# A reserve of filler work, and a later start of the filler, in the attention of a two-layer decoder

## The chip, the cores and the metric

The program runs on one core of one Trainium2 chip. The metric is the device time of one execution in microseconds (us). A core has five engines that work beside each other: TensorE (PE in the profile, with PEld for its weight loads) for matrix products and transposes into PSUM, VectorE (DVE), ScalarE (ACT), GpSimd (POOL) and SyncE (SP), which here only issues DMAs. Each engine takes its instructions strictly in the order in which the built program lists them; a waiting instruction holds up all that stands behind it on its engine.

## The reference

Two decoder layers over 1024 tokens of width 1024, in float32. Layer 0 mixes with retention and mLSTM heads, layer 1 with sparse attention (16 heads in 4 groups) and an S5 state-space branch. Around them:

```
for i in range(DEPTH):
    u = rmsnorm(h, norm_pre[i])
    y = ab_mixer(u, ...) if i % 2 == 0 else cd_mixer(u, ...)
    h = h + rmsnorm(y, norm_post[i])
    h = h + jax.nn.sigmoid(h @ pe_gate[i]) * (p[i] @ pe_proj[i])

def cd_mixer(...):
    y_nsa = nsa(...) * silu(nz)             # compressed, selected and sliding-window attention
    y_s5 = s5(...) * silu(sz)               # s5 ends in z1 * sigmoid(z2), (z1, z2) = y @ w_glu
    mix = concat([y_nsa, y_s5])
    return mix @ w_out                      # cd_w_out, 1536 x 1024
```

The change is about `p[1] @ pe_proj[1]` (below: p Wp), which depends on inputs alone, and about when it and the other products around the attention are computed.

## The kernel before

Every float32 product is made of three: an operand is split into a high and a low part, and TensorE multiplies high by high, high by low and low by high (`mm`, L139, is the line of nearly all matmuls, so tiles tell them apart).

**The attention of layer 1** is a loop over 32 units, a unit being a group of four heads and one tile of 128 tokens: group 0 from tile 7 down to 0, groups 1 and 2 from 0 to 7, group 3 in the order `LAST` = 7, 6, 5, 0, 1, 2, 3, 4. A unit makes scores (`sc`, L1425 takes mask and maximum on VectorE, L1428 the exponential on ScalarE, L1440 and L1442 scale on ScalarE, VectorE or GpSimd), then values: for each 128 keys four transposes (`pt`, L1485), a high part (`pthh`, ScalarE L1476), a low part (`pthl`, VectorE L1477) and two products into `av`. The unit's end takes `av` out through ScalarE and VectorE (L1654, L1655) and multiplies it with the gate `zn`.

**The filler** is a Python generator, `filler`, whose steps are put between the attention's instructions, behind the matmul named by `pace` and at a lower priority; a scheduler then fixes each engine's order. `step(gg, n)` adds `share[gg] * n / 66` to a credit and takes a step of the filler for each whole credit; a group's shares are thus its number of steps. In order, the steps are:

- the S5 branch's GLU: 16 steps of 24 matmuls 256 wide (`gl`);
- the S5 half of the output product (`W2` rows from 1024): 16 steps of 12 matmuls 512 wide (`fp`), stored to `yD`;
- p Wp: per token tile a step that loads 128 rows of p and transposes them (`ft`, two transposes, split by ScalarE L1497 and VectorE L1498), and two steps of 6 `fp` matmuls, copied by ScalarE (L1571) and stored to `ppD`, which only the gate stage reads;
- the output product of groups 0 and 1 (16 steps of 12 `fp`), then of group 2 (16 steps of 6 `fp`), added to `yD`; a step whose attention output isn't there yet is a bare `yield`, which costs a credit and does nothing;
- the **last chain**, for tiles 7, 6, 5, 0, 1, 2, 3: load the two halves of `yD` (L1587), two products of 6 `fp` with group 3's output, VectorE adds each (L1592), ScalarE squares it (L1593), VectorE and GpSimd (L226) make the norm's factor, ScalarE scales (L1601), GpSimd multiplies by the norm's gain (L1602) and adds the residual (L1603) for each half, and SyncE stores to `hD` (L1604).

All filler products go through one PSUM buffer (`pF`), so a product waits until the one before has been read. Results go through a ring of four half tiles (tag `fo`), other inputs through another ring of four (`fin`).

**The gate stage** follows: its weights, its tile loads `h<-hD` (L934; the first two are issued from ScalarE's queue), transposes `trp`, products `gp`, and p Wp read back from `ppD`.

Of the kernel before, what the change touches and what calls it, by code (L numbers as in the profile page):

```python
# [97 lines left out]
def body(tc, A, out, dbg=None):  # L98
# [1058 lines left out]
    with ExitStack() as e:  # L1157
# [252 lines left out]
        pace = [None]  # L1410
# [55 lines left out]
    with ExitStack() as e:  # L1466
# [23 lines left out]

        def filler():

# [26 lines left out]

            wg = weights(A["s5_w_glu"][0], 0, 4)  # L1520
            for l0 in range(0, 8, 2):
                hi = pf.tile([128, 4, 256], FR, name="fhi", tag="fhi")
# [5 lines left out]
                for m in range(4):  # L1528
# [16 lines left out]
                    yield  # L1545
            for src, w, kt0, nk, dst, add in ((None, W2, 8, 4, yD, False),
                                              (A["p"][1, 0], A["pe_proj"][1], 0, 2, ppD, False),
                                              (mixN, W2, 0, 4, yD, True),
                                              (mixN, W2, 4, 2, yD, True)):
                wq = weights(w, kt0, nk)  # L1550
                for i in range(NT):
                    while src is mixN and not all((q, i) in ready for q in ((0, 1) if kt0 == 0 else (2,))):
                        yield
                    x = ftile()
                    to = dst[i * 128:(i + 1) * 128, :]
                    if src is None or src is mixN:
                        x = x.rearrange("p (a k) -> p a k", a=4)[:, :nk]
                        if src is None:
                            to = dst.rearrange("(k l) c -> l k c", l=8)[i]
                            nc.sync.dma_start(x, mixS[:, i, :].rearrange("(a p) k -> p a k", p=128))  # L1560
                        else:
                            nc.sync.dma_start(x, mixN[kt0:kt0 + nk, :, i * 128:(i + 1) * 128].rearrange("a p k -> p a k"))
                        T = local_parts(x, nk, g)
                    else:
                        nc.sync.dma_start(x[:, :nk * 128], src[i * 128:(i + 1) * 128, :])
                        T = turn(x, nk)
                        yield
                    for hf in range(2):
                        hs = slice(hf * 512, (hf + 1) * 512)
                        y = ftile("fy", "fo")  # L1570
                        s.activation(y, product(T, wq[hf], nk), AF.Copy, scale=0.25 if src is None else 1.0)  # L1571
                        if add:
                            y0 = ftile()
                            nc.sync.dma_start(y0, to[:, hs])
                            g.tensor_tensor(y, y, y0, op=OP.add)
                        nc.sync.dma_start(to[:, hs], y)
                        yield
            wq = wlast[0] = [[load_w(W2, [(hf * 512, 512)], 6, 2)] for hf in range(2)]
            for i in LAST[:-NL]:
                while (3, i) not in ready:  # L1580
                    yield
                rows = slice(i * 128, (i + 1) * 128)
# [23 lines left out]

        wlast = [None]
        fill = filler()

        credit = [0.0]  # L1610
        share = {0: 30, 1: 26, 2: 20, 3: 64}
        ready = {}

        def step(gg, n):
            credit[0] += share[gg] * n / 66
            while credit[0] > 0.99:
                credit[0] -= 1
                with tc.issue_after(pace[0].ins), tc.high_priority(offset=FOFF):
                    next(fill, None)

        FOFF = -1000
        for n, (gg, i) in enumerate(units):
# [36 lines left out]
            ready[gg, i] = zt  # L1659
        for _ in fill:  # L1660
            pass
    ep.close()
# [66 lines left out]
```

## Time and profile before

| | us |
|---|---|
| runs, undisturbed | 2359.98, 2362.42, 2365.99 (median 2362.42) |
| the profiled execution | 2361.37 |
| its span in the profile | 2359.5 |
| TensorE busy | 2272.2 (96%) |
| VectorE busy | 1468.9 (62%) |
| ScalarE busy | 1073.5 (45%) |
| GpSimd busy | 488.4 (21%) |

The attention's units run from 1512 to 2241 us of the span, the gate stage from 2250 to the end. The granted clock of TensorE has two levels in the profile, 1.00 (2.4 GHz) and 0.50 (1.2 GHz). A matmul's listed duration includes its way through the array, so a row of matmuls is read by the distance of their starts.

### The profile page before, as it was taken

The page shows a single profiled execution, that of the slowest core. Times are in us where ns is not written, and L with a number is a line of the kernel's source. Part 1 is how long each engine was busy: PE and PEld are TensorE (multiplying, and loading weights), DVE is VectorE, ACT ScalarE, POOL GpSimd, SP SyncE. Part 2 cuts the span into 40 slices and gives each one's busy share as a digit, 9 for nine tenths or more (in the row PEclk, how much of TensorE's full clock was granted, in tenths as well). Part 3 has the DMA queues.
Part 4 walks back from the last instruction along what each step waited for, and adds up shares of the span by engine and source line. Part 5 has one row for each costly group of instructions (what it writes and reads, how often), then busy time and mean ns, then how long its engine had stood idle before and what let it go on. Part 6 is the DMA issues. An engine that isn't in the chain of part 4 may idle for free.

```text
span 2359.5 us, 34480 instructions
## 1 busy us (share of the span) xinstructions
PE 2272.2 (96%) x11974; PEld 1903.7 (81%) x11974; DVE 1468.9 (62%) x3893; ACT 1073.5 (45%) x2345; POOL 488.4 (21%) x585
## 2 busy tenths in 40 slices
PE   7999999999999999999999999989999989999888
PEld 6888889788888788888888899778888778787667
DVE  6777646755554434443287344278787898888833
ACT  6223323433332432233332233267787777787821
POOL 0222200000000000200000000044444245565700
PEclk9999999999999999999999999999999999999999
DMA  6423312021221645424377424342453433355543
GB/s 160 91 78 107 97 50 72 19 72 29 79 72 37 213 156 198 146 77 138 108 221 239 121 80 141 102 135 71 117 164 116 125 110 105 115 171 156 174 160 111
DMA packets 266695, 279.26 MB, mean 118 GB/s; under 512 B 54384, under 2 KB 200408, under 8 KB 266490
## 3 DMA queue, kind: packets, MB, share of 16 engines
q1 hardware_dynamic: 254666, 243.95, 34.1%
q10 hardware_dynamic: 8240, 24.20, 3.1%
q0 software_dynamic: 3616, 8.92, 1.4%
q8 instruction: 95, 1.56, 0.3%
q14 instruction: 78, 0.64, 0.1%
HBM read 189.84 MB, written 88.42 MB: 118 GB/s over the span
## 4 chain that ended last, share of the span: by engine, by line
PE 83%; DVE 7%; DMA 4%; ACT 2%; issue 2%; SPq 1%; POOL 1%; ACTq 0%; DVEq 0%; POOLq 0%
PE pj L139 42%; PE gp L139 7%; PE op L139 6%; PE fp L139 5%; PE av L139 4%; PE sc L139 4%; PE pt L1485 3%; PE yp L139 2%; PE gl L139 2%; DVE pr L1425 1%; PE trp L214 1%; PE pp L139 1%; DVE pthl L1477 1%; PE cs L139 1%; PE hp L139 1%
## 5 line engine op out<-in xcount | busy, mean ns | idle before, releaser
L139 PE MATMUL pj<-whi,uh 128*128 128x512 f32 (+2 forms) x768 | 278.7, 364 | 2.4 <-DVE z L484 0.9
L139 PE MATMUL pj<-wlo,uh 128*128 128x512 f32 (+2 forms) x768 | 277.9, 362 | 0.0
L139 PE MATMUL pj<-whi,ul 128*128 128x512 f32 (+2 forms) x768 | 277.7, 362 | 0.0
L1428 ACT ACTIVATE pr<-pr,nm 128x640 f32<-128x640 f32 (+7 forms) x256 | 187.3, 732 | 66.4 <-DVE nm L1425 63.6
L139 PE MATMUL pj<-vh,whi 128*128 128x512 f32 x512 | 203.9, 399 | 0.2 <-ACT vh L218 0.2
L139 PE MATMUL pj<-vl,whi 128*128 128x512 f32 x512 | 201.3, 393 | 0.0
L139 PE MATMUL pj<-vh,wlo 128*128 128x512 f32 x512 | 201.1, 393 | 0.0
L164 DVE SCALAR_TENSOR_TENSOR wlo<-raw,gnp,whi 128x256 fp32r<-128x256 f32 (+3 forms) x264 | 144.8, 586 | 75.3 <-ACT whi L163 74.5
L1477 DVE TENSOR_TENSOR pthl<-pt,pthh 128x512 fp32r<-128x512 f32 x264 | 177.4, 683 | 16.3 <-ACT pthh L1476 14.1
L163 ACT ACTIVATE whi<-raw,gnp 128x256 fp32r<-128x256 f32 (+3 forms) x264 | 138.0, 585 | 79.6 <-PE pj L139 38.3
L139 PE MATMUL op<-whi,mhl 128*128 128x512 f32 x520 | 165.4, 395 | 2.7 <-ACT mhl L218 1.9
L1476 ACT ACTIVATE pthh<-pt 128x512 fp32r<-128x512 f32 x264 | 149.8, 592 | 37.4 <-PE pt L1485 34.5
L139 PEld LDWEIGHTS pj<-whi,uh 128*128 128x128 f32 x768 | 145.6, 190 | 25.7 <-PE trp L214 1.1
L1485 PE MATMUL pt<-consts,pr 128*128 128x128 f32 x1056 | 161.8, 277 | 4.3 <-ACT pr L1440 2.1
L139 PEld LDWEIGHTS pj<-wlo,uh 128*128 128x128 f32 x768 | 145.7, 190 | 22.7 <-issue 0.7
L139 PEld LDWEIGHTS pj<-whi,ul 128*128 128x128 f32 x768 | 145.4, 189 | 22.4 <-issue 0.2
L139 PE MATMUL gp<-whi,mhl 128*128 128x512 f32 x480 | 155.3, 399 | 0.0
L1485 PEld LDWEIGHTS pt<-consts,pr 128*128 128x128 f32 x1056 | 130.8, 142 | 28.5 <-ACT pr L1440 3.1
L139 PE MATMUL sc<-kh,q 128*128 128x320 f32 (+5 forms) x384 | 141.4, 371 | 9.2 <-DVE nm L1425 7.7
L1442 POOL TENSOR_SCALAR pr<-pr,cf 128x640 f32<-128x640 f32 (+4 forms) x64 | 114.8, 1793 | 154.9 <-DVE cf L1437 65.3
L139 PE MATMUL sc<-kl,q 82*128 82x320 f32 (+5 forms) x384 | 126.9, 333 | 0.0
L139 PE MATMUL av<-pthl,vt 128*128 128x512 f32 x264 | 115.0, 436 | 9.8 <-DVE pthl L1477 9.4
(444 smaller groups left out, 5546.5 us busy)
## 6 DMA issues: line engine op xcount, KB each, us to landing
raw<-in_ab_w_in_dram SPq DMA_DIRECT2D x100, 256.0 KB
raw<-in_cd_w_in_dram SPq DMA_DIRECT2D x30, 512.0 KB
yD<-fy SPq DMA_DIRECT2D x48, 256.0 KB
raw<-in_ab_w_out_dram SPq DMA_DIRECT2D x16, 512.0 KB
raw<-in_pe_gate_dram SPq DMA_DIRECT2D x16, 512.0 KB
qD<-qst SPq DMA_DIRECT2D x16, 512.0 KB
q<-qD SPq DMA_DIRECT2D x32, 256.0 KB
fin<-yD SPq DMA_DIRECT2D x32, 256.0 KB
```

The costliest lines, as they stand in the source:

```text
L139: return t.matmul(o, l, r, start=start, stop=stop, **k)
L163: s.activation(hi[:, k], raw[:, k], AF.Copy, scale=gain(kt0 + k))
L164: v.scalar_tensor_tensor(lo[:, k], raw[:, k], gain(kt0 + k), hi[:, k].bitcast(FT), op0=OP.mult, op1=OP.subtract)
L214: t.transpose(ps[:, k * 128:(k + 1) * 128], x[:, (k4 + k) * 128:(k4 + k + 1) * 128], ident)
L1425: v.tensor_tensor_reduce(pr[:, x:y], ps[:, :y - x], mask[:, x:y], op0=OP.add, op1=OP.min, scale=-1.0, scalar=nm[:, 0:1] if c else 3e38, ac ...
L1428: s.activation(pr[:, :nk], pr[:, :nk], AF.Exp, scale=-1.0, bias=nm[:, c:c + 1], accum_out=sums[:, b, h:h + 1])
L1442: (v if eng == "v" else g).tensor_scalar(P[h][:, :nk], P[h][:, :nk], cf[:, h:h + 1], None, op0=OP.mult)
L1476: s.activation(hi[:dst_shape], ps[:dst_shape], AF.Copy)
L1477: v.tensor_tensor(lo[:dst_shape], ps[:dst_shape], hi[:dst_shape].bitcast(FT), op=OP.subtract)
L1485: t.transpose(ps[:, h * 128:(h + 1) * 128], P[h][:, k * 128:(k + 1) * 128], ident)
```

## The change

The filler becomes two generators. `filler(True)`, the reserve (`extra`), has p Wp alone; `filler()` has the rest. The transposing step of p Wp loses its own `yield`, so a tile of p Wp is two steps. Where the main filler's inputs are missing it now yields `False`: no credit is spent on that, and `step` instead takes two steps of the reserve for two credits, if the main filler has come to its narrow weights (those of group 2's product, `nk == 2`) or the reserve has begun; if the reserve can't be drawn on, the loop stops and the credit is kept. The credit starts at -2.5, and the shares of the four groups go from 30, 26, 20, 64 to 20, 16, 18, 53. What is left of both generators runs after the loop.

```
-        def filler():
+        def filler(spare=False):
...
-            wg = weights(A["s5_w_glu"][0], 0, 4)
-            for l0 in range(0, 8, 2):
+            wg = None if spare else weights(A["s5_w_glu"][0], 0, 4)
+            for l0 in range(0, 0 if spare else 8, 2):
...
-            for src, w, kt0, nk, dst, add in ((None, W2, 8, 4, yD, False),
-                                              (A["p"][1, 0], A["pe_proj"][1], 0, 2, ppD, False),
-                                              (mixN, W2, 0, 4, yD, True),
-                                              (mixN, W2, 4, 2, yD, True)):
+            for src, w, kt0, nk, dst, add in (((A["p"][1, 0], A["pe_proj"][1], 0, 2, ppD, False),) if spare else
+                                              ((None, W2, 8, 4, yD, False), (mixN, W2, 0, 4, yD, True),
+                                               (mixN, W2, 4, 2, yD, True))):
                 wq = weights(w, kt0, nk)
+                narrow.append(nk == 2)
                 for i in range(NT):
                     while src is mixN and not all((q, i) in ready for q in ((0, 1) if kt0 == 0 else (2,))):
-                        yield
+                        yield False
...
                         T = turn(x, nk)
-                        yield
...
+            if spare:
+                return
             wq = wlast[0] = [[load_w(W2, [(hf * 512, 512)], 6, 2)] for hf in range(2)]
             for i in LAST[:-NL]:
                 while (3, i) not in ready:
-                    yield
+                    yield False
...
-        wlast = [None]
-        fill = filler()
-
-        credit = [0.0]
-        share = {0: 30, 1: 26, 2: 20, 3: 64}
+        wlast, narrow = [None], []
+        fill, extra = filler(), filler(True)
+
+        credit = [-2.5]
+        share = {0: 20, 1: 16, 2: 18, 3: 53}
...
         def step(gg, n):
+
             credit[0] += share[gg] * n / 66
             while credit[0] > 0.99:
+                with tc.issue_after(pace[0].ins), tc.high_priority(offset=FOFF):
+                    if next(fill, False) is False:
+
+                        if not any(narrow) or next(extra, False) is False or next(extra, False) is False:
+                            break
+                        credit[0] -= 1
                 credit[0] -= 1
-                with tc.issue_after(pace[0].ins), tc.high_priority(offset=FOFF):
-                    next(fill, None)
...
-        for _ in fill:
-            pass
+        for x in (fill, extra):
+            for _ in x:
+                pass
```

In the changed kernel's listing the lines of the filler move down by one or two: L1497 and L1498 become L1498 and L1499, L1509 becomes L1510, L1587 to L1604 become L1589 to L1606, L1654 becomes L1661.

**The start of the filler, ScalarE.** The values of the first unit (`pthh`), with the first inputs of the GLU (`fin`) ahead of them. Before:

```order
L1440 ACTIVATE pr<-pr,cf 128x1024
L1134 ACTIVATE zt<-pj 128x512
L159 ACTIVATE whi<-raw 128x1024 x2
L1370 ACTIVATE scc<-scc 128x4x48
L1497 ACTIVATE fhi<-fin 128x4x128 x2
L1476 ACTIVATE pthh<-pt 128x512 x3
```

And now:

```order
L1440 ACTIVATE pr<-pr,cf 128x1024
L1134 ACTIVATE zt<-pj 128x512
L159 ACTIVATE whi<-raw 128x1024 x2
L1370 ACTIVATE scc<-scc 128x4x48
L1498 ACTIVATE fhi<-fin 128x4x128 x2
L1476 ACTIVATE pthh<-pt 128x512 x3
```

Nothing has moved here but a line number. On TensorE at this place the first `gl` matmuls go from the first unit's values to behind them.

**The end of the attention, TensorE.** The last product of the last unit and what follows it (`trp` and `gp` are the gate stage's). Before:

```order
L139 MATMUL av_23343<-pthl_23450,vt_19023 128x512
L214 MATMUL trp_23531<-consts_75,h1_23528 128x128 x4
L214 MATMUL trp_23538<-consts_75,h1_23528 128x128 x4
L139 MATMUL gp_23579<-whi_23481,mhl_23530 128x512
L139 MATMUL gp_23579<-wlo_23482,mhl_23530 128x512
```

And now, where `fp_22830` is the first of five products of the last chain:

```order
L139 MATMUL av_23198<-pthl_23334,vt_18848 128x512
L139 MATMUL fp_22830<-whi_21553,fhi_22720 128x512
L139 MATMUL fp_22830<-wlo_21554,fhi_22720 128x512
L139 MATMUL fp_22830<-whi_21553,flo_22721 128x512
L139 MATMUL fp_22830<-whi_21553,fhi_22720 128x512
```

All 30 matmuls of those five products follow the last `av`, then five times two `ft` and 12 `fp`, and only then `trp`.

**The same place, ScalarE.** Before, from the last `av` being taken out (`oc`) to the first loads of the gate stage:

```order
L1654 ACTIVATE oc_23455<-av_23343 64x256
L1601 ACTIVATE fy_23242<-fy_23242,rsb_23325 128x512
L1601 ACTIVATE fy_23243<-fy_23243,rsb_23325 128x512
L934 DMA h1_23528<-hD2_98 128x1024
L934 DMA h1_23545<-hD2_98 128x1024
```

And now the end of the last chain (tile 3) and the first of the five reserve tiles:

```order
L1595 ACTIVATE fin_23175,ms2_23105<-fy_23098 128x512
L1603 ACTIVATE fy_23097<-fy_23097,rsb_23180 128x512
L1603 ACTIVATE fy_23098<-fy_23098,rsb_23180 128x512
L1498 ACTIVATE fhi_23260<-ft_23257 128x2x128
L1571 ACTIVATE fy_23264<-fp_23265 128x512
L1571 ACTIVATE fy_23274<-fp_23275 128x512
```

Four more reserve tiles (L1498 and two of L1571 each) and two weight splits (L159) follow before the two loads of L934.

## Rows read from the trace of the kernel before

**Rows 1.** Busy time by stretch: attention by groups, group 3 in two parts.

```profile
core 0: us, PE busy (x) PEld busy (x) DVE busy (x) ACT busy (x) POOL busy (x), PEclk, DMA share, GB/s
1512.00:1721.00 209.00, 193.88 (x1241) 170.83 (x1239) 159.33 (x485) 141.73 (x322) 87.96 (x87) 0.96 0.42 118
1721.00:1898.00 177.00, 170.61 (x957) 143.50 (x957) 144.36 (x451) 135.91 (x294) 65.94 (x70) 0.99 0.40 124
1898.00:2074.00 176.00, 164.50 (x902) 133.55 (x901) 156.57 (x451) 133.56 (x271) 90.81 (x88) 0.99 0.35 109
2074.00:2157.00 83.00, 79.69 (x452) 68.33 (x451) 68.70 (x194) 66.33 (x144) 54.32 (x49) 0.96 0.54 166
2157.00:2241.00 84.00, 71.15 (x355) 55.31 (x354) 73.65 (x211) 67.75 (x161) 60.04 (x60) 0.94 0.56 175
```

**Rows 2.** TensorE's waits from 1480 to 2250: total us, times, longest.

```profile
PE sc L139 <- DVE nm L1425: 7.7, 18, 1.1
PE cs L139 <- DMA q<-qD: 6.8, 7, 1.7
```

**Rows 3.** Timeline at the first unit's values: start, duration, instruction, [idle before].

```profile
1554.62 0.63 ACT L1497 ACTIVATE fhi<-fin 128x512 fp32r<-128x512 f32 x1 [3.13 <-DMA fin<-y5D]
1555.96 1.56 ACT L1476 ACTIVATE pthh<-pt 128x512 fp32r<-128x512 f32 x3
...
1556.60 0.79 PE L139 MATMUL av<-pthh,vt 128*128 128x512 f32 x1 [7.81 <-ACT pthh L1476]
```

**Rows 4.** Chain of waits: filler matmuls in an unbroken row (start, us).

```profile
1584.79 2.50 PE gl L139 x21
...
1733.20 2.77 PE fp L139 x12
```

**Rows 5.** Timeline of TensorE near the end of the last unit.

```profile
2228.72 0.66 PE L139 MATMUL av<-pthl,vt 128*128 128x512 f32 x1 [2.27 <-DVE pthl L1477]
2229.18 0.63 PE L139 MATMUL av<-pthh,vt 128*128 128x512 f32 x1
...
2234.25 1.25 PE L1485 MATMUL pt<-consts,pr 128*128 128x128 f32 x10
...
2250.15 1.97 PE L214 MATMUL trp<-consts,h 128*128 128x128 f32 x8 [9.09 <-DMA h<-hD]
```

**Rows 6.** Timeline of ScalarE at the same place (ACTq is its DMA issue).

```profile
2245.88 2.29 ACTq L934 DMA_DIRECT2D h<-hD  x2
```

**Rows 7.** The reserve's own work by tile: ns min/median/max, first and last start.

```profile
L1509 PE MATMUL ft<-consts,fin x16: 270/272/293, 1812.5 to 1901.1; 128*128 128x128 f32 x16
L1497 ACT ACTIVATE fhi<-ft x8: 362/371/414, 1813.9 to 1902.5; 128x256 fp32r<-128x256 f32 x8
L1498 DVE TENSOR_TENSOR flo<-ft,fhi x8: 383/416/425, 1814.6 to 1904.2; 128x256 fp32r<-128x256 f32 x8
L1571 ACT ACTIVATE fy<-fp x64: 572/597/616, 1716.7 to 2148.0; 128x512 f32<-128x512 f32 x64
```

**Rows 8.** The last chain's work by line, same columns.

```profile
L1592 DVE TENSOR_TENSOR fy<-fy,fp x14: 668/684/689, 2158.0 to 2240.0; 128x512 f32<-128x512 f32 x14
L1602 POOL TENSOR_TENSOR fy<-fy,fin x14: 1263/1292/1307, 2168.8 to 2248.6; 128x512 f32<-128x512 f32 x14
L1603 POOL TENSOR_TENSOR fy<-fy,fin x14: 1261/1290/1383, 2172.7 to 2249.9; 128x512 f32<-128x512 f32 x14
L1498 POOL TENSOR_TENSOR flo<-zn,fhi x7: 725/734/852, 2148.2 to 2232.2; 128x256 fp32r<-128x256 f32 x7
L226 POOL TENSOR_TENSOR rsb<-rsa,mhalf x32: 550/552/731, 6.4 to 2314.9; 128x1 f32<-128x1 f32 x32
```

**Rows 9.** Chain of waits: the last chain's store and reload (start, us).

```profile
2216.85 5.45 DMA hD<-fy
2222.32 2.76 DMA fy<-yD
```

**Rows 10.** Busy time in a stretch inside rows 5, columns as rows 1.

```profile
2229.00:2232.00 3.00, 3.00 (x11) 2.17 (x11) 3.00 (x5) 1.62 (x3) 2.81 (x2) 0.50 0.92 259
```

## The prediction

> **What bounds the kernel now.** I read the busy time of the five engines by group of units first [rows 1]. In the attention TensorE is busy in 679.8 of 729 us. It stands idle for 15.1, 6.4, 11.5 and 16.2 us in groups 0 to 3, 49.2 us in all, while VectorE is busy for 602.6 us (83%). So TensorE sets the pace, VectorE is close behind it, and a microsecond of filler taken out of a stretch saves at most a microsecond there. Then I read what ends the idle time. Most waits are short ones on the attention's own data: the maxima of the scores, 7.7 us in 18 waits, and the loads of q, 6.8 us in 7 [rows 2]. One is long: at 1548.8 TensorE stops for 7.81 us, since ScalarE waits for the GLU's first input and the first unit's high parts stand behind that conversion in its queue [rows 3]. Last I read the end: after the last product of the last unit TensorE waits 9.09 us for the gate stage's first tile [rows 5], whose load ScalarE issues at 2245.88 [rows 6].
>
> The work itself is the same before and after: the same matmuls in another order. So the sum has three places: the start, the inside of the attention, and the stretch from the last `av` to the first `trp`.
>
> **The start: nothing.** The filler's first matmuls now come behind the first unit's values, but what stopped TensorE was ScalarE's conversion of the first GLU input, and this stands in front of `pthh` exactly as before, with the same load issued at the same place. I leave the 7.81 us where it is. If the load should come some us earlier, the gain would be at most those 7.8 us.
>
> **Inside the attention: 27 us less.** The filler's matmuls by group, counted in the two orders, each in a row 0.119 us (2.50/21) for `gl` and 0.231 us (2.77/12) for `fp` [rows 4], 0.11 us for a transpose ((1.25 - 0.27)/9) [rows 5]:
> - group 0: 384 `gl` and 19 `fp` become 360 and 0: -7.2 us of TensorE;
> - group 1: 257 `fp` and 14 `ft` become 24 `gl` and 180 `fp`: -16.5 us;
> - group 2: 204 `fp`, 2 `ft` become 216 `fp`: +2.6 us;
> - group 3 up to the last `av`: 180 `fp` become 174 and 6 `ft`: -0.7 us.
>
> That is 21.8 us, and it is what now stands behind the last `av`: 90 `fp` (five products of the last chain, ten of the reserve) and 10 `ft`, 20.8 + 1.1 us. In groups 0 and 1 VectorE is at 76% and 82% [rows 1]; with 7 and 16 us less the second goes to 90%, so nine tenths of the cut should show: -6 and -15. In group 2 the added filler fits into idle time, and the new bookkeeping puts it at units that had none: -1. In group 3 two and a half tiles of the last chain leave, with VectorE's two additions of 0.684 us and GpSimd's 6.4 us for each (2 x 1.292 + 2 x 1.290 + 0.734 + 0.552) [rows 8], in a stretch where TensorE was idle for 12.9 of 84 us: -5. Together -27. If VectorE hides half of the cut in groups 0 and 1 it is -14; if besides the whole 21.8 a third of the 41.4 us of idle time outside the 7.81 us goes away, it is -36.
>
> **Behind the last `av`: 53 us more.** Here nothing covers the filler, and it is a chain, since all products share one PSUM buffer and ScalarE takes its work in order: the first reserve tile's conversion stands behind the scaling of the last chain's last tile, and the gate stage's loads stand behind the last copy of the reserve.
> - The last chain. By the order, when the last `av` ends GpSimd is about to begin with the fourth of the seven tiles, and the fifth and sixth follow. At 6.4 us a tile it comes to the factor of the seventh after about 19 us, and ScalarE's two scalings of it follow, 20.6 us. But a half tile can be loaded only when the one four earlier in the ring is stored, a store of 5.45 and a load of 2.76 us on the chain of waits [rows 9]; one such round trip shows once, less what GpSimd does meanwhile, 5 to 6 us. I take 26 us. The ends are GpSimd alone, 20.6, and the pace at which these tiles left before, from 2168.8 to 2249.9 14 halves or 11.6 us a tile [rows 8], 29 us for two and a half.
> - Five reserve tiles. Each: two transposes 0.38, high part 0.37, low part 0.42, product 1.55 (five starts and one whole matmul of 0.39), copy 0.60, product 1.55, copy 0.60 [rows 4, 7], 5.5 us, and seven hand-overs of about 0.1 us: 6.1. Five are 30.5 us, 27.4 without the hand-overs.
> - Then a weight split of about 1 us on ScalarE, the load (issued at 2245.88, `trp` at 2250.15: 4.3 us) [rows 5, 6].
>
> 26 + 30.5 + 1 + 4.3 = 61.8 us from the last `av` to `trp`, where 9.1 were: +52.7. The low end is 20.6 + 27.4 + 5.3 - 9.1 = +44. What would have to hide it isn't there: the gate stage's matmuls stand behind the last reserve product on TensorE, and its tiles aren't loaded.
>
> **The sum.** 2361.4 (the profiled run) - 27 + 52.7 = 2387.1. The profiled run lies 1.0 under the median of the runs shown, so 2388 on their scale. The gate stage itself keeps its order and its waits.
>
> **Rivals.**
>
> *TensorE's clock stays low in the new tail.* In the idle end of the last unit the granted clock went to 0.50, 1.2 GHz, [rows 10], and starts of a 512-wide product lay 0.46 us apart instead of 0.23 [rows 5]. In the reserve's stretch TensorE would work 3.5 of 6.1 us, in pieces of 1.5 us between waits of about 1 us; in the stretch from 2157 on it was busy for 85% and had a mean of 0.94 [rows 1]. At the low level each of the ten products takes 1.4 us more and the transposes some 0.2 a tile: +15, so 2403. Against it: the waits are shorter than those before the spells of low clock in the attention. For it: nowhere in this trace is TensorE so thinly used for 30 us.
>
> The Trainium skill, TensorE: Matmul & The Clock Gate, section "A second HAM failure mode: psum-queue depth-cycling", says that small gaps between groups of matmuls, made by cycling through PSUM, can make the clock go back and forth between its two levels, so that work is lost though no single gap is long. By that rule the reserve through one buffer would run at the low level for part of its time, and 2403 is its time if it does so throughout; the trace has the low level in short spells only (means of 0.94 to 0.99 by group), so it stays the second case.
>
> *The even spread wins (the other side).* The thinner filler and the reserve at the places with missing inputs take the idle time out of the attention, all 41.4 us of it beside the 21.8 us of moved work: -63.2, and with the same tail 2362.4 - 63.2 + 52.7 = 2352. It decides from the point where the attention loses more than 52.7 us, that is 31 of the 41.4 us. Against it: the named waits [rows 2] end with VectorE's maxima and the loads of q, which the change doesn't touch, and only units 16 to 19 lacked filler for want of input.
>
> *Both ends favourable.* The attention loses 36 and the tail costs 44: +8, so 2370, about the edge of what counts as no change.
>
> *The change doesn't do what it says.* In part this is in the forecast: by the order only three of the eight reserve tiles are drawn before the last `av`, and five are left for the end. There is no further case, since the order is fixed.
>
> **How the numbers follow.** Chances: forecast (2376 to 2397) 0.60; low clock in the tail (2397 to 2415) 0.22; both ends favourable (2362 to 2376) 0.12; even spread (below) 0.06. The predicted time is that of the likeliest, 2388. The range leaves out the even spread, the top of the low clock and the bottom of the favourable case: 2370 to 2410. 0.3%, about what a measurement of this kernel can tell from no change, is 7.1 us. Slower by more than that: 0.60 + 0.22 + half of 0.12 and a bit, 0.89; within it 0.06; faster 0.05.
>
> **What would show it.** In the profile of the changed kernel: the wait of 7 to 8 us before the first unit's `av` still there; groups 0 and 1 some 6 and 15 us shorter; between the last `av` and the first `trp` about 62 us, in which five `ft` pairs stand 6 to 7.5 us apart, VectorE is nearly idle and the gate stage's first load is issued only after the last `fp`; the first `ft` of that row some 26 us behind the last `av`. The prediction is wrong if the last chain's three tiles are through in 15 us, if the attention's idle time falls below 20 us, or if the reserve's tiles take 4 us each.

## The result, and the profile after

The changed kernel takes 2425.7 us (median of four runs, 2418.1 to 2430.8) beside 2361.2 us for the kernel before on the same chip: a ratio of 1.0265, 95% interval 1.0239 to 1.0291. The direction was forecast, the size was not: +64 us where +26 was expected, 16 us above the top of the range (2410), and above all four cases that the forecast names.

The profiled run of the change took 2418.1 us, 56.8 us more in span than the profiled run before. It splits like this, with the forecast beside it:

| stretch | before | after | difference | forecast |
|---|---|---|---|---|
| up to the first unit's first `av` | 1511.9 | 1517.3 | +5.4 | 0 |
| attention, first to last `av` | 729.1 | 707.1 | -22.0 | -27 |
| last `av` to first `trp` | 9.1 | 79.4 | +70.3 | +52.7 |
| gate stage, first `trp` to the end of the engines' last instruction | 105.6 | 108.4 | +2.8 | 0 |

The first difference lies in a stretch that the change doesn't touch; over the kernels below the first `av` begins between 1509.3 and 1517.3. After the last row of the table the program runs on for about 4 us in both kernels, without an engine at work. The busy time by stretch, columns as in [rows 1]: the four groups, and the tail in two parts (last chain, reserve):

```profile
core 0: us, PE busy (x) PEld busy (x) DVE busy (x) ACT busy (x) POOL busy (x), PEclk, DMA share, GB/s
1517.00:1711.00 194.00, 180.57 (x1176) 157.82 (x1174) 151.57 (x465) 131.05 (x299) 75.67 (x79) 0.98 0.39 109
1711.00:1876.00 165.00, 160.01 (x915) 132.44 (x913) 145.52 (x455) 132.17 (x287) 70.94 (x73) 0.99 0.37 109
1876.00:2064.00 188.00, 175.22 (x937) 143.15 (x936) 167.43 (x475) 140.44 (x287) 102.43 (x96) 0.95 0.40 122
2064.00:2224.00 160.00, 145.21 (x782) 118.88 (x781) 131.40 (x383) 124.36 (x284) 86.46 (x87) 0.95 0.45 142
2224.00:2260.00 36.00, 13.52 (x32) 7.99 (x31) 7.28 (x15) 10.89 (x24) 21.25 (x20) 0.64 0.65 211
2260.00:2304.00 44.00, 28.77 (x71) 17.42 (x72) 2.12 (x5) 9.78 (x17) 6.40 (x4) 0.62 0.29 97
```

Groups 0 and 1 are shorter than in [rows 1] by 15 and 12 us, group 2 is longer by 12, group 3 shorter by 7. The last two rows are new: no engine is busy for more than two thirds of either, and the granted clock is 0.64 and 0.62. What TensorE waited for in these 80 us (total us, times, longest):

```profile
PE fp L139 <- DVE fy L1594: 12.1, 5, 5.6
PE ft L1510 <- DMA fin<-in_p_dram: 8.3, 1, 8.3
PE fp L139 <- DVE flo L1499: 4.7, 5, 0.9
PE trp L214 <- DMA h<-hD: 4.0, 1, 4.0
PE fp L139 <- ACT fy L1571: 3.5, 5, 0.7
PE ft L1510 <- ACT fy L1571: 2.8, 4, 0.7
PE fp L139 <- POOL flo L1499: 2.4, 1, 2.4
```

The five lines with `fy` or `flo` are hand-overs between the steps of the last chain and of the reserve; the forecast had these steps in its sum, though with fewer waits for loads in the first line than came. The second line, 8.3 us for the first reserve tile's own load, it did not have. The timeline shows where that load was held (SPq is the queue's issue):

```profile
2248.38 0.69 DVE L1594 TENSOR_TENSOR fy<-fy,fp 128x512 f32<-128x512 f32 x1 [6.17 <-DMA fy<-yD]
2254.67 1.33 ACT L1603 ACTIVATE fy<-fy,rsb 128x512 f32<-128x512 f32 x2 [1.04 <-POOL rsb L226]
2253.66 0.32 SPq L1602 DMA_DIRECT2D fin<-hD  x1
2256.75 2.53 POOL L1604 TENSOR_TENSOR fy<-fy,fin 128x512 f32<-128x512 f32 x2 [2.11 <-DMA fin<-in_norm_post_dram]
2258.04 4.55 SPq L1566 DMA_DIRECT2D fin<-in_p_dram  x4
2260.32 0.66 PE L1510 MATMUL ft<-consts,fin 128*128 128x128 f32 x2 [8.28 <-DMA fin<-in_p_dram]
```

The last tile of the last chain holds all four `fin` buffers with its two gains (of the norm) and two residuals (the load at 2253.66 is the last of them). GpSimd's multiplication at 2256.75 frees the first one, only then is a `p` load issued (2258.04), and the first transposes follow at 2260.32. So the reserve stood behind GpSimd's work on the last tile, not behind ScalarE's scaling, which was through at 2256.0.

One reserve tile in the chain of waits (start, duration, step, matmuls):

```profile
2269.14 0.70 PE ft L1510 x2
...
2269.86 0.39 ACT fhi L1498
...
2270.28 0.43 DVE flo L1499
...
2270.75 2.94 PE fp L139 x6
...
2273.77 0.61 ACT fy L1571
...
2274.42 2.94 PE fp L139 x6
...
2277.43 0.61 ACT fy L1571
...
2278.09 0.70 PE ft L1510 x2
```

It is the chain of the forecast, step by step, but a product takes 2.94 us instead of 1.55, and the tile 8.95 us instead of 6.1: the clock is at 0.50, 1.2 GHz, from 2244.1 to 2291.9.

### The profile page after: what moved, and what is told of

Same layout as the page of the kernel before. It is cut to its first block, busy times and chain, and to the rows that moved or that the text cites. A ratio compares the mean times of both kernels' runs of the same rounds, so it can differ in the third digit from the quotient of the medians.

```text
span 2416.3 us, 34547 instructions
## 1 busy us (share of the span) xinstructions
PE 2296.7 (95%) x11974; PEld 1911.5 (79%) x11974; DVE 1469.7 (61%) x3893; ACT 1073.8 (44%) x2345; POOL 485.9 (20%) x585
## 4 chain that ended last, share of the span: by engine, by line
PE 83%; DVE 7%; DMA 5%; ACT 2%; issue 2%; SPq 1%; POOL 1%; DVEq 0%; ACTq 0%; POOLq 0%
PE pj L139 41%; PE op L139 7%; PE gp L139 7%; PE fp L139 5%; PE av L139 4%; PE sc L139 4%; PE pt L1485 3%; PE yp L139 2%; DVE pr L1425 2%; PE gl L139 1%; DVE pthl L1477 1%; PE trp L214 1%; PE pp L139 1%; PE cs L139 1%; PE hp L139 1%
## 5 line engine op out<-in xcount | busy, mean ns | idle before, releaser
L1476 ACT ACTIVATE pthh<-pt 128x512 fp32r<-128x512 f32 x264 | 149.5, 591 | 34.3 <-PE pt L1485 26.6
L139 PE MATMUL sc<-kh,q 128*128 128x320 f32 (+5 forms) x384 | 141.2, 370 | 10.3 <-DVE nm L1425 8.9
```

Of the source, the lines that this page charges most:

```text
L139: return t.matmul(o, l, r, start=start, stop=stop, **k)
L1476: s.activation(hi[:dst_shape], ps[:dst_shape], AF.Copy)
```

## The experiments

The theory after the result (A): the loss is the serial tail; it came out larger than forecast because the reserve and the last chain share the ring of loads, and because TensorE's clock is low there. The rivals, run by run, are that the thin pace loses (the smaller shares, which put off work), that the reserve loses by itself, and that the hand-overs make a tile slow whatever the clock. Times are medians, each ratio is to the kernel before, run beside it on the same chip; attention is first to last `av`, tail is last `av` to first `trp`, both from the profiled run.

| run | time, us | ratio to before | attention | tail |
|---|---|---|---|---|
| before | 2361 | | 729.1 | 9.1 |
| the change | 2425.7 | 1.0265 | 707.1 | 79.4 |
| e1_g3_share | 2403.2 | 1.0169 | 745.3 | 35.1 |
| e2_old_shares | 2379.5 | 1.0075 | 745.5 | 5.3 |
| e3_own_ring | 2391.4 | 1.0118 | 714.6 | 48.5 |
| e4_busy_pe | 2423.3 | 1.0252 | 716.0 | 78.2 |
| e5_late_credit | 2368.1 | 1.0035 | 727.9 | 14.9 |
| e6_before_ring6 | 2358.7 | 0.9990 | 721.7 | 7.9 |
| e7_old_shares_own_ring | 2373.9 | 1.0057 | 747.2 | 5.1 |
| e8_split_tile | 2383.6 | 1.0107 | 753.5 | 6.0 |
| e9_own_loads | 2390.1 | 1.0126 | 714.9 | 48.4 |
| e10_own_results | 2416.4 | 1.0239 | 712.8 | 75.5 |
| e11_own_psum | 2378.2 | 1.0069 | 732.8 | 20.5 |
| e12_no_reserve | 2344.8 | 0.9939 | 717.8 | 5.2 |

**The ring: three runs.** Separate buffers for both kinds of the reserve's tiles, for its loads alone, for its results alone:

```diff
-                return pf.tile([128, 512], FT, name=name, tag=tag, bufs=4)
+                return pf.tile([128, 512], FT, name=name, tag=tag + "s" * spare, bufs=2 if spare else 4)
```

In e9 the condition is `spare and tag == "fin"`, in e10 `spare and tag == "fo"`.

> The changed kernel, but the reserve's loads and results have buffers of their own (two each) instead of four shared with the last chain. By the order only one product (6 fp) of the last chain now stands behind the last av, then the five reserve tiles as before. Theory A (the last chain lost its time to the shared ring: the p load waited for the last chain's inputs to be read, the last tile's loads for stores): the first ft comes 10 to 16 us sooner after the last av (20 to 26 instead of 35.9), reserve tiles 9 us each as before: 2408 to 2416. Rival (the last chain goes at the pace of GpSimd and of its loads, whatever the ring): first ft within 4 us of 35.9, 2421 or more.

> The changed kernel with buffers of their own (two) for the reserve's loads alone; its results still share four with the last chain. By the order one product of the last chain stands behind the last av, as in the run where both were apart (2391). Theory A (the loads are what couples the two: a reserve tile's load waits for the last chain's inputs to be read, and the last chain's for the reserve's): 2386 to 2397, first ft 6 to 12 us behind the last av. Rival (the results couple them): 2415 or more.

> The changed kernel with buffers of their own (two) for the reserve's results alone. TensorE's order is that of the changed kernel to the last row. Theory A (the loads couple them): the change's own time, 2418 to 2431, first ft 33 to 37 us behind the last av; it is then at the same time a second profile of the change's own order. Rival (the results couple them): 2386 to 2400.

Two load buffers give back 35.6 us (e9), and with the results apart as well 34.3 us (e3). With the results alone apart the time is 9.3 us under the change's at the same order on TensorE (e10), a little under theory A's 2418; the intervals of the two ratios overlap (1.0220 to 1.0257 and 1.0239 to 1.0291). So the loads couple the two chains. With load buffers of its own the order on TensorE is another too: four of the five left products now go ahead of the last `av` and cost 7 to 8 us there (714.6 and 714.9 against 707.1; 2 against e10's 712.8). e3's expectation knew that order, and its 2408 to 2416 was still missed by 17 us: the first `ft` comes 8.0 us behind the last `av` (8.2 in e9, 35.9 in the change, 34.9 in e10) where 20 to 26 were expected, and the tiles are faster than the 9 us expected.

The same runs price the clock. The starts of e9's five tiles lie 7.6, 6.2, 6.1 and 8.0 us apart, those of e10 7.6, 6.2, 6.1 and 8.2, those of the change 8.8, 8.9, 8.9 and 7.6. The busy time of e10 in the stretches with the tiles one, two and three, and four and five (columns as above, the clock third from the end):

```profile
2262.00:2270.00 8.00, 5.28 (x15) 3.19 (x15) 0.42 (x1) 1.58 (x3) 1.93 (x2) 0.67 0.51 166
2270.00:2282.00 12.00, 7.48 (x28) 4.57 (x28) 0.85 (x2) 2.92 (x6) 0.00 (x0) 1.00 0.23 87
2282.00:2299.00 17.00, 12.32 (x28) 7.40 (x28) 0.85 (x2) 3.97 (x8) 2.27 (x1) 0.57 0.17 62
```

The middle row has two tiles at a clock of 1.00 in 12 us; the last has two in 17 us at 0.57. The same instructions with the same hand-overs take 6.1 to 6.2 us a tile at the high level, and 8.8 to 8.9 in the change, where the low level lasts; tiles of 7.6 to 8.2 us have both. That speaks against the rival that the hand-overs alone make a tile slow. e10 is also a second profile of the change's order on TensorE: its tail was 75.5 us with the clock back at full for 17 us of it, that of the change 79.4.

**The tail taken away: two runs.** The share of the last group raised, so that the reserve is drawn before the last `av`; and the shares of before with the reserve (the first two lines are e1, the others e2).

```diff
-        share = {0: 20, 1: 16, 2: 18, 3: 53}
+        share = {0: 20, 1: 16, 2: 18, 3: 76}
...
-        credit = [-2.5]
-        share = {0: 20, 1: 16, 2: 18, 3: 53}
+        credit = [0.0]
+        share = {0: 30, 1: 26, 2: 20, 3: 64}
```

> The changed kernel with the last group's share raised from 53 to 76, so that all eight reserve tiles are drawn in front of the last av; behind it stand only the five products (30 fp) of the last chain, no ft. The groups before are paced as in the changed kernel. Theory A (the loss is the serial tail, last chain and five reserve tiles): last av to first trp falls from 79.4 us to about 42 (36 us of last chain plus 6 for the gate stage's load), group 3 takes back 60 fp and 10 ft, 15 us of TensorE, of which 5 to 15 us show: 2395 to 2405. Theory B (the thin pace of the early groups is what costs, the tail only shows work put off): the whole stays at 2418 or more. Theory C (the tail is paid by the reserve alone, the last chain would hide): tail near 15 us and a time under 2380.

> The changed kernel's reserve with the shares of before (30, 26, 20, 64) and a credit that begins at 0; nothing of the filler stands behind the last av, 16 ft and all 96 fp of the reserve in front of it. Theory A (the pace made the tail, and the reserve itself is harmless): no tail (9 to 12 us from av to trp), attention as before, 729 us within 10, so 2352 to 2372. Theory B (drawing p Wp late, in groups 2 and 3, costs by itself, since its tiles share ring and PSUM buffer with the last chain): 2380 or more. Theory D (the reserve at places with missing input takes idle time out of groups 2 and 3): the 9.9 us more filler in group 1 and 5 less in group 2 leave a time under 2352.

e1's tail is 28.0 us of last chain and 7.1 of load, 35.1 where 42 were expected, and the time lies in theory A's range. But the last group grew from 160.8 to 196.4 us for 15 us of moved work. Its units 29 and 30:

```profile
2163.00:2208.00 45.00, 34.92 (x164) 25.80 (x162) 26.98 (x88) 27.66 (x63) 10.65 (x11) 0.96 0.32 100
2208.00:2247.00 39.00, 28.17 (x117) 20.80 (x118) 15.22 (x37) 20.52 (x40) 15.20 (x12) 0.89 0.42 135
```

TensorE is idle for 10 to 11 us in each and VectorE is at 60% and 39%. The reserve stands there in pieces of several products in a row, with the same waits of 0.69 and 0.93 us as in the tail: inside the attention such a piece is the same chain where no other work stands between its steps.

e2 has no tail at all, 5.3 us, and is still slower than before by 0.75% (0.48 to 1.01%), between both theories:

```profile
1512.00:1718.00 206.00, 192.09 (x1242) 169.21 (x1241) 160.13 (x486) 141.85 (x323) 88.05 (x87) 0.98 0.43 120
1718.00:1919.00 201.00, 193.04 (x1031) 163.21 (x1031) 145.65 (x440) 138.53 (x295) 92.77 (x90) 0.96 0.43 129
1919.00:2097.00 178.00, 162.84 (x895) 132.43 (x894) 159.57 (x475) 140.46 (x290) 86.42 (x89) 0.97 0.39 123
2097.00:2258.00 161.00, 143.89 (x738) 116.66 (x737) 138.37 (x396) 126.86 (x288) 93.06 (x88) 0.90 0.46 145
```

With the reserve out of the stream, group 1 draws 341 `fp` instead of 257, and 84 fewer are left for groups 2 and 3. Group 1 grows by 24 us, and groups 2 and 3 give back only 4 together. Of the 16.3 us that the attention lost, TensorE's busy time is 11.6 and its idle time 4.7: the same matmuls ran longer, since the clock was at its low level for 65 us of the attention instead of 41 (0.90 in the last row). An estimate from the traces bears this out. A 512-wide matmul starts 0.23 us after the one before it at the high level and 0.43 to 0.46 at the low one, so take half of the busy time spent at the low level as lost: without it the attention's work on TensorE is 663.3 us in the kernel before and 663.0 in e2. It holds beyond one profile: the mean clock of the whole run was 0.979 to 0.983 in the four runs of e2, and 0.985 to 0.990 in the seven of the kernel before beside them.

**Why the reserve costs inside: two runs.** The kernel of e2 with buffers apart, as in e3, and the kernel of e2 with a reserve tile drawn in three single steps, with a high and a low part of its own:

```diff
                         T = turn(x, nk)
+                        yield
...
-                        if not any(narrow) or next(extra, False) is False or next(extra, False) is False:
+                        if not any(narrow) or next(extra, False) is False:
                             break
-                        credit[0] -= 1
```

> The reserve with the shares of before and a credit from 0 (as the run with the old shares, 2379.5), and buffers of its own for the reserve's loads and results. Theory A (the reserve costs inside the attention because its loads and results share four buffers with the last chain and the yD products): 2360 to 2370. Rival B (it costs because a tile goes as a chain of transposes, conversions, product, copy, product, with one PSUM buffer, in one piece; the ring has nothing to do with it): 2374 to 2384, and single units of groups 2 and 3 with waits of 0.7 and 0.9 us at ft and fp as in the tail.

> The reserve with the shares of before and a credit from 0, the ring shared as in the changed kernel, but a reserve tile in three steps, drawn one by one as in the kernel before (transposes, first product, second product), with a high and a low part of its own. Theory B (a reserve tile in one piece makes TensorE wait for its conversions and copies): 2360 to 2370, the waits before the reserve's first products gone or under 0.3 us. Rival A (the ring) and rival C (it is the pace: 18 us more filler in group 1, less in groups 2 and 3, so that VectorE's stretches in groups 2 and 3 have less beside them and the clock falls more often): 2374 or more.

e7's 2373.9 us lies 4 us above theory A's range and just under rival B's, 5.6 us under e2 (the intervals overlap) with an attention that is no shorter. e8 is 4.2 us over e2, in the range of A and C. The waits that B names were not there to be taken away: in e2's own trace TensorE never waits more than 0.14 us before the transposes or the two products of a reserve tile, in e8 0.15 us before the products. Neither the ring nor the single piece explains the cost with the shares of before; what stays, because the others fell, is e8's rival C, the pace. Two things in the traces fit it. TensorE's waits for the attention's own maxima grew from 7.7 us in 18 to 12.8 in 22 (e2), 15.3 in 27 (e7) and 15.8 in 31 (e8), and those for the loads of q from 6.8 us to 10.9, 10.3 and 10.2. And over the kernels with all the filler inside the attention, TensorE's busy time there goes with the time at the low level: 675.2 us busy with 31 us at the low level (e6), 680.0 with 41 (before), 691.6 with 65 (e2), 696.2 with 68 (e8), 696.9 with 79 (e7), some 0.45 us for each. Without half of the busy time at the low level, as above, they come to 664.2 (e6), 663.3, 663.0, 667.3 (e8) and 663.0 us (e7). Why the clock is low for longer in e2, e7 and e8 was not tried by itself.

**The later begin.** The kernel before with one number changed:

```diff
-        credit = [0.0]
+        credit = [-2.5]
```

> The kernel before with one number of the change alone: the credit begins at -2.5, so the filler's matmuls begin later and one product (6 fp) of the last chain is left behind the last av. Theory A (the later begin gains nothing by itself: the conversion of the GLU's first input stays in front of the first unit's high parts, and what is put off is paid at the end): the idle time of 7 to 8 us behind the first unit stays, the tail grows by 2 to 10 us, the attention is within 10 us of 729: 2360 to 2375. Rival (the begin behind the first unit's values takes the start's idle time away): that wait under 2 us and a time of 2350 to 2358.

Theory A: the wait behind the first unit is there as before (7.66 us), one product stands behind the last `av`, the tail is 14.9 us, and the kernel is slower by 0.35% (0.19 to 0.50%).

**A longer ring in the kernel before.**

```diff
-                return pf.tile([128, 512], FT, name=name, tag=tag, bufs=4)
+                return pf.tile([128, 512], FT, name=name, tag=tag, bufs=6)
```

> The kernel before with six buffers instead of four for the filler's loads and as many for its results. Theory A (in the kernel before the last chain has the attention's matmuls as cover, so a longer ring gains nothing but the round trip at the very end): 2355 to 2365, the wait before trp 5 to 9 us. Rival (the ring holds the filler up inside the attention too): under 2352.

Theory A, 0.999 (0.998 to 1.000): in the kernel before, where the attention covers the last chain, the ring of four costs next to nothing. It is the fastest kernel with the whole computation, by hardly more than can be measured.

**The clock by added work.** In the drain behind the loop:

```diff
+                if warm[0]:
+                    dm = pT.tile([128, 512], FT, name="dm", tag="pt")
+                    proj_tok(dm, T, 0, ck, 512, nkt=1)
```

and eight transposes behind a tile's two.

> The changed kernel with matmuls added that nobody reads, only in the drain behind the loop: eight transposes behind a reserve tile's two, three matmuls behind each product, so that TensorE has work while ScalarE and VectorE convert. Three to four of the five leftover tiles get them. Theory A (the low granted clock, 0.50 in the whole stretch, is what made a tile cost 9.0 us instead of 6.1 to 7.5): the granted clock goes to 1.0 within the reserve, those tiles take 6.0 to 7.5 us: 5 to 10 us off, 2416 to 2421. Rival (the hand-overs make the 9 us, the clock is only a sign): the tiles take 9 to 11 us, and the time is 2425 or more.

This run decided nothing: 2423.3 us, between the two ranges, and tiles 9.0, 8.2, 9.0 and 7.4 us apart, one of them at full clock. The order had put the added matmuls behind other products than their own, they filled some gaps and lengthened other steps, and a tile of 7.4 us at full clock carries its own added work. The price of the clock comes from e9 and e10.

**The PSUM buffer.** e3 with the reserve's transposes and products in the three buffers of the attention's transposes:

```diff
-                ps = pF.tile([128, 512], FT, name="fp", tag="pf")
+                ps = (pT if spare else pF).tile([128, 512], FT, name="fp", tag="pt" if spare else "pf")
```

and the same for `ft`.

> The run with loads and results apart (2391.4) once more, but the reserve's transposes and products also go to the three PSUM buffers of the attention's transposes instead of the one of the filler. By the order four reserve tiles stand behind the last av, the next tile's transposes in front of this one's second product. Theory A (a tile is a chain because all its steps share one PSUM buffer, and the clock is low because of the gaps in it): tiles 3.5 to 4.5 us apart, gaps of 0.7 us gone, granted clock 1.0 in them; 36 us for five tiles become 14 to 20 for four, and the time 2368 to 2380. Rival (ScalarE's queue and the conversions set the pace, whatever the buffers): tiles 6 us or more apart, 2385 or more.

TensorE's waits from 2247 to 2268 (total, times, longest), and two stretches of the busy time:

```profile
PE trp L214 <- DMA h<-hD: 5.0, 1, 5.0
PE fp L139 <- ACT fhi L1498: 2.5, 4, 0.8
```

```profile
2251.00:2258.00 7.00, 5.96 (x27) 4.42 (x26) 0.85 (x2) 2.61 (x6) 0.00 (x0) 1.00 0.46 167
2258.00:2263.00 5.00, 3.79 (x17) 2.58 (x15) 0.42 (x1) 2.44 (x5) 0.00 (x0) 1.00 0.28 105
```

The first two lines are TensorE's waits in the tail, the others the busy time there. Theory A: the waits for `fy` are gone, four of up to 0.8 us for the conversions stay, the tiles follow at 5.4 and 4.0 us, the clock is 1.00, the tail is 20.5 us instead of 48.5, and the time lies in theory A's range. But it fell by 13 us, not 28: the attention grew by 18 us for one more reserve tile and one more product of the last chain (18 `fp`, 2 `ft`, 4.4 us) inside it. Of the 18 us 9.9 are busy time and 8.2 idle; why was not tried. A microsecond that leaves the tail isn't a microsecond won.

**Without the reserve.**

```diff
                     if next(fill, False) is False:
-                        if not any(narrow) or next(extra, False) is False or next(extra, False) is False:
-                            break
-                        credit[0] -= 1
+                        break
```

with the drain of `extra` left out and `pp` read from `hD[1]`.

> The changed kernel's pace without the reserve: the second layer's p Wp is left out, and the gate stage reads the same number of bytes of another array in its place. 96 fp and 16 ft are gone, 22.2 + 1.8 = 24 us of TensorE. By the order nothing of the filler stands behind the last av. Theory A (the reserve costs more than its work, by the serial tail and by putting the last chain off): last av to trp 5 to 9 us, attention 695 to 705, the time 2325 to 2340, that is some 90 us under the change for 24 us of work. Rival (the thin pace alone has made the tail): tail 25 us or more, 2360 or more.

The four groups:

```profile
1512.00:1710.00 198.00, 184.79 (x1172) 162.04 (x1171) 151.60 (x464) 131.36 (x299) 75.25 (x79) 0.95 0.38 107
1710.00:1878.00 168.00, 163.19 (x916) 135.32 (x916) 144.27 (x454) 132.11 (x285) 70.81 (x74) 0.97 0.35 106
1878.00:2066.00 188.00, 176.78 (x941) 144.86 (x940) 166.89 (x476) 141.73 (x289) 101.07 (x97) 0.95 0.39 122
2066.00:2230.00 164.00, 145.91 (x770) 117.69 (x768) 142.74 (x393) 127.86 (x295) 108.07 (x103) 0.96 0.53 168
```

2344.8 us, 5 us above theory A's range, far under the rival's, and 81 us under the change for 24 us of TensorE's work. The tail is 5.2 us, as theory A has it: without the reserve the last chain too is through when the attention ends, so the thin pace alone does not make the tail. The attention is 717.8 us where 695 to 705 were expected, and that is the second finding of this run: against the kernel before it has 24 us less filler, but TensorE's busy time fell only from 680.0 to 670.4 us, with 65 us at the low level instead of 41.

## Why the prediction was off

The outline was right: a serial tail that nothing covers and that costs more than the attention gains. Two terms of the tail were too small by 9 to 10 us each: the last chain, where the sum counted one round trip of loads and left out that the reserve's loads share a ring with it, and the five reserve tiles, which the sum priced at the high clock. The attention gave 5 us less than forecast, and stretches put at nothing added 8.

**The start: right.** The wait is 7.84 us (7.81 before [rows 3]), and e5 (7.66) shows that the later begin alone doesn't move it.

**Attention, -27: too hopeful.** The profile shows -22.0; e10, the same order on TensorE, has 712.8 us, -16.3. By groups -6, -15, -1, -5 were forecast, and -15, -12, +12, -7 came (e10: -12, -9, +11, -7). The limits between groups move with the change: group 2 holds 276 `pt` and 208 `sc` instead of 268 and 198. The sum over groups is clean, the parts are not. The step that failed is "nine tenths of the cut should show", which took VectorE as the only thing that can eat the gain. In e10 the clock ate it: the idle time fell by 6.7 us, more than the 5 of the forecast, but busy time fell only by 9.6 of the 21.8 us of work, with the low level for 68 us instead of 41; half of the busy time at that level, 27.9 us against 16.7, is 11 of the 12 us missing (the estimate used for e2). e12 shows the same: 24 us of work cut, 9.6 us of busy time back, 65 us at the low level. The profiled run of the change is not explained this way: with 44 us at the low level its busy time fell by 18.9 us, but its idle time only by 3.2, and what kept the rest was not found. The -14 that the forecast gives for a VectorE that hides half of the cut does not come out of its own terms (half of -6 and -15, with -1 and -5, is -16.5); nothing else was built on it.

**The last chain, 26: measured 35.9 to the first `ft`, 34.9 in e10.** Two parts of the term were mis-sized. The chain itself: ScalarE's scaling of the last tile ended 31.6 us behind the last `av`, not 26, since VectorE waited 2.6, 2.4 and 6.2 us for `fy<-yD` loads where one round trip [rows 9] was counted:

```profile
2223.94 0.50 PE L139 MATMUL av<-pthl,vt 128*128 128x512 f32 x1
2229.33 0.69 DVE L1594 TENSOR_TENSOR fy<-fy,fp 128x512 f32<-128x512 f32 x1 [2.58 <-DMA fy<-yD]
2240.03 0.69 DVE L1594 TENSOR_TENSOR fy<-fy,fp 128x512 f32<-128x512 f32 x1 [2.42 <-DMA fy<-yD]
```

The third and longest of these waits is in the timeline of the result. The other part is the reserve's begin: the first transposes were taken to be done by then, waiting for ScalarE; they came 4.3 us after the scaling's end, held by their load. The forecast let a load wait for a buffer in the ring of results ("a half tile can be loaded only when the one four earlier in the ring is stored"), but not in the other ring, `fin`, which the reserve's loads share with the last chain's gains and residuals. e9, with two load buffers for the reserve, has its first `ft` 8.2 us behind the last `av` and a time 35.6 us lower; since the order on TensorE changed with it, that is more than the price of this one wait. The low price named in the forecast, 20.6, holds for GpSimd alone and was never near.

**Five reserve tiles, 30.5: measured 39.5, 36.3 in e10.** The 6.1 us a tile is right at full clock, 6.1 and 6.2 us in e9 and e10. The rest is the clock, which the forecast had as a rival with 0.22: at its low level a product took 2.94 instead of 1.55 us, +1.4 as that rival priced it, and a tile 8.9. So the rival and the forecast were not two cases but one: the gaps were in the forecast, and the clock that came with them in every run with such a tail (low for at least part of it) belonged into the same sum. With the rival's +15 in the likeliest case the forecast would have been 2403, with the longer last chain 2413.

The Trainium skill, TensorE: Matmul & The Clock Gate, section "A second HAM failure mode: psum-queue depth-cycling", was cited for that rival: small gaps from cycling through PSUM cost work though none is long. The runs agree in direction: gaps of 0.7 to 0.9 us through one PSUM buffer, and the low level for 47.8 us in the change; with three buffers and without most of those gaps 1.00 (e11). They also show that the outcome isn't fixed by the gaps: e10 has the same ones, and full clock for 17 us among them.

**The load, 5.3: measured 4.0. The gate stage, 0: measured +2.8.** The "weight split of about 1 us" was one of three. ScalarE issues the tile's load at 2299.91, but stands 5.62 us for the gate's next weights with the tile's conversions queued behind them, and TensorE's first `gp` waits 2.84 us for these. ScalarE's timeline of the change:

```profile
2299.91 0.82 ACTq L934 DMA_DIRECT2D h<-hD  x2
...
2307.07 1.06 ACT L159 ACTIVATE whi<-raw 128x1024 fp32r<-128x1024 f32 x1 [5.62 <-DMA raw<-in_pe_gate_dram]
2308.03 1.06 ACT L218 ACTIVATE mhl<-trp 128x512 fp32r<-128x512 f32 x2
```

Of the kernels here, those whose tail ends with reserve tiles through the filler's one PSUM buffer (the change, e3, e4, e9, e10) have a wait of 2.8 to 3.0 us there, the kernel before has none.

**The rivals that fell.** The even spread didn't win: the attention's idle time is 46.0 us against 49.2. Waits with VectorE's maxima are 8.9 us in 20 where 7.7 in 18 stood [rows 2], as the argument against that rival said. The case with both ends favourable had the tail at +44, where +70.3 came.

**The profiled run and the median.** The profiled run of the change is the fastest of its four, 7.6 us under their median, and had the highest clock, a mean of 0.974 over the run; the two runs of 2430.8 us had 0.967 and 0.969. A forecast from one profile carries such a spread on both sides.

Together on the profile: last chain +9.9, reserve +9.0, load -1.3, attention +5.0, the stretches outside +8.2, against 2387.1: 2417.9, where 2418.1 was measured. These are all readings of one trace, so that they add up proves nothing about the causes; the tail's two causes rest on e3, e9, e10 and e11.

## What to carry to other kernels

Work kept in reserve is cheap only while something else stands between its steps. The same 24 us of p Wp cost 81 us here, nearly all of it in the tail: 39.5 us where the reserve ran alone, as a chain through one PSUM buffer, and 35.9 where the last chain, put off for its sake, ran ahead of it and held its loads. Before costing a tail, list each ring, PSUM buffer and queue that its parts share, and price the first load of the second chain as waiting for the last read of the first; two load buffers gave back 35.6 of the 64.5 us lost. And cost thin stretches of TensorE at the low clock as the likeliest case, in the tail and in the attention: in e12 24 us less filler shortened the attention by 11 us.

## What the runs showed of the chip beyond that

- TensorE's granted clock differs between runs of one order: 44 us of the attention at the low level in the change, 68 in e10, with 661.1 and 670.4 us busy. Between kernels of the same work (before, e2, e6, e7, e8) one us more at the low level went with some 0.45 us more of busy time.
- In the change it stayed at 0.50 for 47.8 us without a break, from the last tile of the last chain through three reserve tiles, in which TensorE was busy for 6.5 to 6.6 of each 9 us; in e10 it stayed at 1.00 for 17 us with the same instructions and the same waits.
